# Scaling the attention probabilities inside their transposes: a diagonal right factor in place of row scalings

## The chip, the core and the metric

The kernel runs on one core of one Trainium2 chip. Its engines each work through a queue of their own in the order in which the program was built: TensorE (PE, with its weight loads shown apart as PEld), VectorE (DVE), ScalarE (ACT), GpSimd (POOL) and SyncE (SP), which issues most DMAs. An engine waits where an operand is not ready, and everything behind the waiting instruction waits with it. The metric is the device time of one execution in microseconds (us), median of three; lower is better.

## The reference

A sequence of 512 tokens of width 1024 goes through three layers in float32. The first has two kinds of attention (MLA with 8 heads, and SWA with 8 heads over a sliding window of 128), the second has 16 heads of attention with a forget bias (called "fox" below), and both are followed by a layer norm, an MLP, another layer norm and a gate. The third layer is gated linear attention and a gated MLP. What the change touches is the softmax of all 32 heads and the product with V:

```python
w = jax.nn.softmax(s, axis=-1).astype(v.dtype)
return jnp.einsum('bhqk,bkhd->bqhd', w, v)
```

## The kernel before

Tokens are cut into four blocks of 128 (`NB` = 4, `P` = 128). Large products run as three multiplies of split float32 (`mm3`: operands typed fp32r, held in the tiles `ar_t` and `ax_r`), while everything in plain float32 lies in `af_t` and `ax_f`. On PE, therefore, a row that names `ar_t` or `ax_r` is an fp32r multiply, a row that names only `af_t` and `ax_f` is a multiply of plain float32, and a row that names `ident` is a transpose (L255).

Each attention head is one generator, `head` (L758). For each block `i` of 128 queries it computes the scores (`smm`, in `layer1` or `layer2`), on DVE their row maximum (L808 or L812), on ACT the exponentials with their row sums `su` (`exps`, L794), and on DVE the reciprocal `rc` (L827). `preg(i)` is the region with the probabilities of query block `i`; it is 128 to 512 columns wide (128 or 256 in SWA). L828 and L829 scale each region by its row's reciprocal, four DVE instructions a head. Then PE transposes the 128x128 pieces of the regions, 7 a head in SWA and 10 a head in MLA and fox, so 8x7 + 8x10 + 16x10 = 296 in all, into two or three PSUM banks (`groups`); ACT alone, or ACT and DVE, copy the banks out (L840 to L846), and PE multiplies by V (L852 or L861). In SWA and MLA this last product is of plain float32, and so are MLA's scores; in fox both are fp32r.

The order on every engine is set when the program is built. `Core` keeps an estimated clock for each engine and estimated ready times for each stretch of memory; each operation is entered through a helper (`mm`, `tr`, `ts`, `tt`, ...) that adds its estimated cost to a clock, and `run` (L375) lets that generator go on whose next PE work is ready by these estimates, with a priority for older heads. A cost that is written differently thus moves instructions everywhere behind it. Buffers come from the arenas `R` (fp32r) and `F` (float32) through `alloc`, which makes a generator wait until there is room.

Of the kernel before, what the change touches and what calls it, by code (L numbers as in the profile page):

```python
# [9 lines left out]
F32 = mybir.dt.float32  # L10
F32R = mybir.dt.float32r
BF16 = mybir.dt.bfloat16
AF = mybir.ActivationFunctionType
ALU = mybir.AluOpType
# [4 lines left out]
NB = 4  # L19
P = 128  # L20
# [123 lines left out]
class Core:  # L144
# [91 lines left out]

    def mm(self, out, lhsT, rhs, start, stop, more=False):
        n = self.size(rhs)
        slow = 4 if rhs.dtype == F32 else 1
        m = self.size(lhsT)  # L240
        if rhs.dtype == F32R:
            cost = max((n + self.edge) / 2.4, 107 * m / 128)
        else:
            cost = slow * max(n / 2.39, 107 * m / (256 if rhs.dtype == BF16 else 128))
        self.op("pe", cost, [lhsT, rhs], [out])
        self.nc.tensor.matmul(out, lhsT, rhs, start=start, stop=stop, **(dict(skip_group_check=True) if more else {}))  # L246

# [307 lines left out]
def model_kernel(ctx: ExitStack, tc: tile.TileContext, a: dict, dbg=None):  # L555
# [13 lines left out]
    R, F = Arena(ar_t, NR), Arena(af_t, NF)  # L569
    c = Core(nc, R, F, Arena(sm_t, NS, 4), ps_t)  # L570
# [7 lines left out]
    def small(n):  # L578
        n4 = -(-n // 4) * 4
        if ring[0] + n4 > NS:  # L580
            ring[0] = 0
        o = ring[0]
        ring[0] += n4
        return sm_t[:, o : o + n]
# [4 lines left out]
    ident = cp.tile([P, P], F32, name="ident")  # L589
# [19 lines left out]
    def tb(t):  # L609
        return slice(t * P, t * P + P)  # L610
# [147 lines left out]
    def head(kind, qk, smm, scale, vst, of, orow, bias=None, init=None, sink=None, free=()):  # L758
# [19 lines left out]
        def preg(i):  # L778
            n, o = place[i]
            return pb[n].ap[:, o : o + width[i]]  # L780
# [5 lines left out]
        ng, su, rc = small(4), small(4), small(4)  # L786
# [16 lines left out]
        for n, bank in enumerate(banks):  # L803
            yield ("x", [c.pb(sb[n])])
            for i in bank:
                if bias is not None:
                    b = bias[:, 256 - width[i] : 256] if swa else bias[:, : width[i]]
# [17 lines left out]
        else:  # L825
            yield ("x", [su])
        c.vec(94, [su], [rc]).reciprocal(rc, su)  # L827
        for i in range(NB):  # L828
            c.ts(preg(i), preg(i), rc[:, i : i + 1])  # L829
        tset = yield from pl[1].get()  # L830
        tbk = []
        for grp in groups:
            yield ("pe", [preg(i) for _, i in grp], True)
            b = c.bank()
            for n, (j, i) in enumerate(grp):
                col = (0 if (j == i - 1 or i == 0) else 128) if swa else j * 128
                c.tr(c.pb(b)[:, n * 128 : n * 128 + 128], preg(i)[:, col : col + 128], ident)
            tbk.append((b, len(grp) * 128))
        pl[0].give(pset)
        for (b, w), tz in zip(tbk, tset):  # L840
            yield ("x", [c.pb(b)])
# [6 lines left out]
        if full:  # L848
            yield ("pe", [tz.ap for tz in tset] + [vst], True)
            b = c.bank()  # L850
# [5 lines left out]
        else:  # L856
            yield ("pe", [z.ap for tz in tset for z in tz[:2]] + [vst], True)
            b = c.bank()
# [121 lines left out]
    def layer1():  # L980
# [117 lines left out]
        def swa_pair(pr, b):  # L1098
            yield ("x", [c.pb(b)])
            of = yield from c.allocs(R, 512, 2)  # L1100
            po = PairOut(4 + pr, None, of)
            kv = pr // 2
            for hh in range(2):
                h = pr * 2 + hh
                qb = yield from c.alloc(R, 512)
                q = qb.ap
                own, oth = hh * 64, 64 - hh * 64
                src = c.pb(b)[own : own + 64]
                c.acopy(q[own : own + 64], src)
                c.tt(q[oth : oth + 64], src, f32(q[own : own + 64]), ALU.subtract)  # L1110

                def smm(out, i, q=q):
                    ks = slice(max(0, i - 1) * 128, i * 128 + 128)
                    c.mm(out, q[:, tb(i)], skh[kv][:, ks], True, False)
                    c.mm(out, q[:, tb(i)], skl[kv][:, ks], False, True)

                def fin(qb=qb, po=po):
                    qb.free()
                    po.one()
                    swa_done()  # L1120

                c.spawn(head("swa", [q, ske, bev], smm, 0.125, vsw[:, :, kv], of, own,
                             bias[:, h], nsink[:, h : h + 1], sink[:, h : h + 1], [fin]), prio())
            c.give(b)
# [72 lines left out]
        def mla_pair(pr, bq, bk):  # L1197
# [4 lines left out]
            for hh in range(2):  # L1202
                h = pr * 2 + hh
                yield ("x", [lambda: bool(kfree)])
                n = kfree.pop(0)
                k = kbb[n].ap
                qb = yield from c.alloc(F, 512)
                q = qb.ap
                rs = slice(hh * 64, hh * 64 + 64)
                rr = slice((h % 4) * 32, (h % 4) * 32 + 32)  # L1210
                c.acopy(k[0:64], c.pb(bk)[rs])
                c.act(q[0:64], c.pb(bq)[rs], AF.Copy, scale=96.0 ** -0.5)
                c.ts(q[64:96], rpb[h // 4].ap[rr], 96.0 ** -0.5)

                def smm(out, i, q=q, k=k):
                    c.mm(out, q[0:96, tb(i)], k[0:96, 0 : i * 128 + 128], True, False)
                    c.mm(out[:, i * 128 : i * 128 + 128], identb, maskb, False, True)

                def fin(qb=qb, n=n, po=po):
                    qb.free()  # L1220
                    kfree.append(n)
                    mla_done[0] += 1
                    po.one()

                c.spawn(head("mla", [q, k], smm, None, vm[:, :, h], of, hh * 64, free=[fin]), prio())
# [440 lines left out]
    def layer2():  # L1666
# [60 lines left out]
        def pair(pr, bq, bk):  # L1727
# [9 lines left out]
            for hh in range(2):  # L1737
# [22 lines left out]
                def fin(z=(qb, kb, lb, nb), po=po):  # L1760
# [3 lines left out]
                    if not vleft[g]:  # L1764
                        vb.free()
                    po.one()

                c.spawn(head("fox", [q, kh, kl], smm, 0.125, vst[:, :, (pr % 2) * 2 + hh], of, own, bias=nb.ap,
                             free=[fin]), prio())
            c.give(bq)  # L1770
# [715 lines left out]
```

## Time and profile before

| | before |
|---|---|
| median of 3 runs | 1842.64 us (1838.52 to 1843.07) |
| the profiled execution | 1841.28 us |
| its span from the first to the last instruction | 1839.6 us |
| PE busy | 1810.7 us (98%) |
| DVE busy | 1165.8 us (63%) |
| ACT busy | 901.0 us (49%) |

An engine's busy time is the union of its instructions' times. The mean time of one PE instruction is longer than its share of the engine, because multiplies overlap in the pipeline; what one costs is read from the distance between starts. In the timeline, instructions of one kind that follow each other are one row with their count, and the time of such a row reaches from the first start to the last end. "PEclk" is the clock granted to TensorE: 1.00 is 2.4 GHz, 0.50 is 1.2 GHz.

### The profile page before, as it was taken

How to read it: one execution, taken by the hardware profiler on the slowest of the kernel's cores; microseconds unless marked ns; L12 is line 12 of the kernel's file. 1: busy time of each engine (PE TensorE's matmuls, PEld its weight loads, DVE VectorE, ACT ScalarE, POOL GpSimd, SP SyncE). 2: the span in 40 equal slices, each digit the busy share in tenths (PEclk: the TensorE clock that was granted, in tenths of full speed). 3: DMA queues.
4: the chain of work that ended last, by engine and by line, in shares of the span. 5: the costliest groups of instructions: out<-in, count | busy, mean ns of one | idle time of the engine just before them, and what ended most of it. 6: DMA issues, size and time to landing. Idle time of an engine off the chain costs nothing. (4 is left out here: it accounts for less than half of the span.)

```text
span 1839.6 us, 23837 instructions
## 1 busy us (share of the span) xinstructions
PE 1810.7 (98%) x9096; PEld 1514.0 (82%) x9096; DVE 1165.8 (63%) x1939; ACT 901.0 (49%) x1594; POOL 141.3 (8%) x227
## 2 busy tenths in 40 slices
PE   9999999999999999999999999999999999999997
PEld 7776798888887888878888888878889898888886
DVE  4557667566568578778765656676675554634646
ACT  4567464545456365555655454563543243333434
POOL 1000011001011000000110100110010000100002
PEclk9999999999999999999999999999999999999999
DMA  5201256463663122323463646441222353633614
GB/s 174 76 32 55 95 183 162 104 193 77 186 137 99 53 93 70 115 69 115 164 168 104 182 93 195 97 142 64 81 92 81 126 189 98 150 125 81 172 24 98
DMA packets 63539, 212.01 MB, mean 115 GB/s; under 512 B 7544, under 2 KB 10160, under 8 KB 63424
## 3 DMA queue, kind: packets, MB, share of 16 engines
q1 hardware_dynamic: 50752, 165.39, 25.9%
q0 software_dynamic: 12672, 45.09, 14.1%
q8 instruction: 71, 1.16, 0.3%
q14 instruction: 44, 0.36, 0.1%
HBM read 208.32 MB, written 2.14 MB: 114 GB/s over the span
## 5 line engine op out<-in xcount | busy, mean ns | idle before, releaser
L246 PE MATMUL ps_t<-ar_t 128*128 128x512 f32 (+4 forms) x6537 | 1387.4, 367 | 9.7 <-DVE ar_t L294 3.3
L246 PEld LDWEIGHTS ps_t<-ar_t 128*128 128x128 f32 x6537 | 1127.5, 189 | 207.2 <-DVE ar_t L285 7.3
L285 DVE TENSOR_TENSOR ar_t<-af_t,ar_t 128x1024 fp32r<-128x1024 f32 (+4 forms) x450 | 457.6, 1034 | 356.1 <-ACT ar_t L274 353.4
L274 ACT CAST ar_t<-af_t 128x1024 fp32r<-128x1024 f32 (+4 forms) x477 | 412.1, 884 | 489.2 <-PE ps_t L246 329.1
L246 PE MATMUL ps_t<-ar_t,ax_r 128*128 128x512 f32 (+3 forms) x979 | 252.2, 387 | 0.4 <-ACT ax_r L274 0.2
L246 PEld LDWEIGHTS ps_t<-ar_t,ax_r 128*128 128x128 f32 (+1 forms) x979 | 180.4, 188 | 37.4 <-issue 1.0
L299 DVE SCALAR_TENSOR_TENSOR af_t<-af_t,ps_t 128x512 f32<-128x512 f32 (+2 forms) x218 | 138.1, 659 | 43.9 <-PE ps_t L246 37.8
L285 DVE TENSOR_TENSOR ar_t<-ps_t,ar_t 128x512 fp32r<-128x512 f32 (+4 forms) x181 | 104.3, 602 | 82.6 <-ACT ar_t L274 81.3
L274 ACT CAST ar_t<-ps_t 128x512 fp32r<-128x512 f32 (+4 forms) x181 | 88.4, 525 | 111.9 <-PE ps_t L246 48.7
L270 ACT ACTIVATE af_t<-af_t 128x512 f32<-128x512 f32 (+3 forms) x144 | 92.2, 643 | 103.5 <-DVE af_t L299 60.1
L285 DVE TENSOR_TENSOR ax_r<-af_t,ax_r 128x1024 fp32r<-128x1024 f32 (+4 forms) x109 | 90.9, 834 | 69.4 <-ACT ax_r L274 68.9
L274 ACT CAST ax_r<-af_t 128x1024 fp32r<-128x1024 f32 (+4 forms) x109 | 80.1, 738 | 86.4 <-PE ps_t L246 55.5
L285 DVE TENSOR_TENSOR af_t<-af_t 128x256 f32<-128x256 f32 (+2 forms) x228 | 99.3, 467 | 4.9 <-ACT af_t L270 2.1
L323 POOL DMA_DIRECT2D af_t<-in_w_down x64 | 55.4, 866 | 551.5 <-DVE ar_t L285 531.1
L246 PE MATMUL ps_t<-ax_r,ar_t 128*128 128x512 f32 (+5 forms) x451 | 97.0, 352 | 0.0
L246 PEld LDWEIGHTS ps_t<-ax_r,ar_t 128*128 128x128 f32 (+1 forms) x451 | 77.2, 187 | 12.2
L274 ACT COPY af_t<-ps_t 128x512 f32<-128x512 f32 (+3 forms) x108 | 58.7, 570 | 39.7 <-PE ps_t L246 25.6
L255 PE MATMUL ps_t<-ident,af_t 128*128 128x128 f32 (+1 forms) x499 | 69.2, 277 | 7.0 <-DVE af_t L299 6.9
L270 ACT ACTIVATE af_t<-af_t,sm_t 128x256 f32<-128x256 f32 (+4 forms) x92 | 60.6, 660 | 29.4 <-DVE sm_t L808 20.9
L255 PEld LDWEIGHTS ps_t<-ident,af_t 128*128 128x128 f32 (+1 forms) x499 | 58.7, 141 | 14.4 <-DVE af_t L299 8.1
L270 ACT ACTIVATE af_t<-ps_t 128x512 f32<-128x512 f32 (+3 forms) x111 | 58.7, 529 | 16.6 <-PE ps_t L246 16.4
L299 DVE SCALAR_TENSOR_TENSOR af_t<-af_t,sm_t 128x1024 f32<-128x1024 f32 x40 | 51.0, 1279 | 20.3 <-POOL sm_t L623 17.5
(99 smaller groups left out, 722.4 us busy)
## 6 DMA issues: line engine op xcount, KB each, us to landing
af_t<-in_w_up SPq DMA_DIRECT2D x64, 512.0 KB, 6.2
af_t<-in_w_down POOLq DMA_DIRECT2D x64, 512.0 KB, 5.5
af_t<-in_w_down SPq DMA_DIRECT2D x48, 512.0 KB, 5.4
af_t<-in_w_ffn_gate SPq DMA_DIRECT2D x22, 512.0 KB, 4.4
af_t<-in_w_ffn_up SPq DMA_DIRECT2D x22, 512.0 KB, 4.5
af_t<-in_w_ffn_down POOLq DMA_DIRECT2D x20, 512.0 KB, 5.5
af_t<-in_ple_w_gate SPq DMA_DIRECT2D x16, 512.0 KB, 3.8
af_t<-in_w_ffn_down SPq DMA_DIRECT2D x15, 512.0 KB, 3.4
```

The lines of the kernel that those rows point to most:

```text
L246: self.nc.tensor.matmul(out, lhsT, rhs, start=start, stop=stop, **(dict(skip_group_check=True) if more else {}))
L255: self.nc.tensor.transpose(out, src, ident)
L270: self.nc.scalar.activation(out, src, func, **kw)
L274: self.nc.scalar.copy(out, src)
L285: self.nc.vector.tensor_tensor(out, a, b, op=op)
L299: self.nc.vector.scalar_tensor_tensor(out, a, s, b, op0=op0, op1=op1)
L323: self.nc.gpsimd.dma_start(out, src, accum_op=ALU.add)
```

## The change

The four row scalings of a head go. In their place a DVE instruction multiplies the 128x128 identity, repeated four times, by the four columns of `rc`, which gives four diagonal matrices in a new buffer `dg` of 512 columns. Each transpose becomes a plain multiply with the same stationary operand (the piece of the probabilities, not scaled) and the diagonal of its query block as the moving operand, so that transposing and scaling are one product. The buffer is freed after the last of them. Besides, the planner's price of a plain float32 multiply in `mm` is written anew: n x 0.84 + 4 ns for n columns, where it was four times the larger of n / 2.39 and 107 m / 128 ns (m is the number of stationary columns).

```diff
     def mm(self, out, lhsT, rhs, start, stop, more=False):
         n = self.size(rhs)
-        slow = 4 if rhs.dtype == F32 else 1
...
-            cost = slow * max(n / 2.39, 107 * m / (256 if rhs.dtype == BF16 else 128))
+            cost = n * 0.84 + 4 if rhs.dtype == F32 else max(n / 2.39, 107 * m / 256)
...
         c.vec(94, [su], [rc]).reciprocal(rc, su)
-        for i in range(NB):
-            c.ts(preg(i), preg(i), rc[:, i : i + 1])
+        dgb = yield from c.alloc(F, 512)
+        dg = dgb.ap
+        c.tt(dgb.v(4), ident.unsqueeze(1).to_broadcast([P, NB, P]), rc.unsqueeze(2).to_broadcast([P, NB, P]), ALU.mult)
         tset = yield from pl[1].get()
         tbk = []
         for grp in groups:
-            yield ("pe", [preg(i) for _, i in grp], True)
+            yield ("pe", [preg(i) for _, i in grp] + [dg[:, tb(i)] for _, i in grp], True)
             b = c.bank()
             for n, (j, i) in enumerate(grp):
                 col = (0 if (j == i - 1 or i == 0) else 128) if swa else j * 128
-                c.tr(c.pb(b)[:, n * 128 : n * 128 + 128], preg(i)[:, col : col + 128], ident)
+                c.mm(c.pb(b)[:, n * 128 : n * 128 + 128], preg(i)[:, col : col + 128], dg[:, tb(i)], True, True)
             tbk.append((b, len(grp) * 128))
+        dgb.free()
         pl[0].give(pset)
```

On DVE, the end of one of the last fox heads' softmax stands like this before (the first two rows are a weight's low part and the sum of a residual):

```order
L285 TENSOR_TENSOR ar_t<-af_t,ar_t 128x1024
L299 SCALAR_TENSOR_TENSOR af_t<-af_t,ps_t 128x512
L827 RECIPROCAL sm_t<-sm_t 128x4
L290 TENSOR_SCALAR af_t<-af_t,sm_t 128x128
L290 TENSOR_SCALAR af_t<-af_t,sm_t 128x256
L290 TENSOR_SCALAR af_t<-af_t,sm_t 128x384
L290 TENSOR_SCALAR af_t<-af_t,sm_t 128x512
```

And now, at the same place:

```order
L284 TENSOR_TENSOR ar_t<-af_t,ar_t 128x1024
L284 TENSOR_TENSOR af_t<-ps_t,af_t 64x512
L298 SCALAR_TENSOR_TENSOR af_t<-af_t,ps_t 128x512
L826 RECIPROCAL sm_t<-sm_t 128x4
L284 TENSOR_TENSOR af_t<-ident,sm_t 128x512
```

One instruction of 512 columns stands where there were four of 128 to 512. (Line numbers shift by one.)

On PE, in layer 1, where the first two SWA heads (and three pieces of a latent vector) are transposed between fp32r multiplies of 384 columns, the order before is:

```order
L246 MATMUL ps_t<-ar_t 128x384 x12
L255 MATMUL ps_t<-ident,ax_f 128x128 x12
L255 MATMUL ps_t<-ident,af_t 128x128 x2
L255 MATMUL ps_t<-ident,ax_f 128x128
L255 MATMUL ps_t<-ident,af_t 128x128 x2
L246 MATMUL ps_t<-ar_t 128x384 x6
L246 MATMUL ps_t<-af_t,ax_f 64x256 x3
L246 MATMUL ps_t<-af_t,ax_f 64x128
```

And now (the rows of 128x128 that name only `ax_f` and `af_t` are the new products with the diagonal; the one with `ident` is a transpose that stays):

```order
L245 MATMUL ps_t<-ar_t 128x384 x6
L245 MATMUL ps_t<-ax_f 128x128 x4
L254 MATMUL ps_t<-ident,ax_f 128x128 x3
L245 MATMUL ps_t<-ax_f 128x128 x3
L245 MATMUL ps_t<-ar_t 128x384 x6
L245 MATMUL ps_t<-ax_f 128x128 x2
L245 MATMUL ps_t<-ax_f,af_t 128x128 x2
L245 MATMUL ps_t<-af_t,ax_f 64x256 x3
L245 MATMUL ps_t<-af_t,ax_f 64x128
```

One stretch of 17 transposes has become several stretches of plain float32 multiplies, with fp32r multiplies between them.

On PE, near the end of layer 2: the rows of 512 columns (`x36` and `x12` before) are the 48 multiplies that project q and k of the last pair of heads but one, the rows of 512, 384, 128 and 256 columns in twos are products with V, and the first row of 128 columns in twos begins this pair's scores. Before:

```order
L246 MATMUL ps_t<-ar_t 128x512 x36
L255 MATMUL ps_t<-ident,af_t 128x128 x20
L246 MATMUL ps_t<-ar_t 128x512 x12
L246 MATMUL ps_t<-ax_r,ar_t 128x512 x2
L246 MATMUL ps_t<-ax_r,ar_t 128x384 x2
L246 MATMUL ps_t<-ax_r,ar_t 128x128 x2
L246 MATMUL ps_t<-ar_t 128x256 x2
L246 MATMUL ps_t<-ar_t 128x512 x2
L246 MATMUL ps_t<-ar_t 128x384 x2
L246 MATMUL ps_t<-ar_t 128x128 x2
L246 MATMUL ps_t<-ar_t 128x256 x2
L246 MATMUL ps_t<-ar_t 128x128 x2
```

And now:

```order
L245 MATMUL ps_t<-af_t 128x128 x20
L245 MATMUL ps_t<-ar_t 128x512 x18
L245 MATMUL ps_t<-ax_r,ar_t 128x512 x2
L245 MATMUL ps_t<-ax_r,ar_t 128x384 x2
L245 MATMUL ps_t<-ax_r,ar_t 128x128 x2
L245 MATMUL ps_t<-ar_t 128x256 x2
L245 MATMUL ps_t<-ar_t 128x512 x2
L245 MATMUL ps_t<-ar_t 128x384 x2
L245 MATMUL ps_t<-ar_t 128x128 x2
L245 MATMUL ps_t<-ar_t 128x256 x2
L245 MATMUL ps_t<-ar_t 128x512 x24
L245 MATMUL ps_t<-ar_t 128x128 x2
```

Here 24 multiplies precede the 20 products with the diagonal, so that 24 + 18 + 6 of the last-but-one row make this pair's projection, and the other 18 of that row are the next pair's; they now stand between the projection and the scores that need it.

## Rows read from the trace of the kernel before

**Rows 1.** The page: span, and busy time by engine.
```profile
span 1839.6 us, 23837 instructions
PE 1810.7 (98%) x9096; PEld 1514.0 (82%) x9096; DVE 1165.8 (63%) x1939; ACT 901.0 (49%) x1594; POOL 141.3 (8%) x227
```

**Rows 2.** Busy us and instructions by stretch: attention of layers 1, 2; an MLP.
```profile
core 0: us, PE busy (x) PEld busy (x) DVE busy (x) ACT busy (x) POOL busy (x), PEclk, DMA share, GB/s
57.00:216.00 159.00, 154.97 (x766) 113.14 (x765) 98.94 (x243) 93.87 (x232) 2.41 (x6) 0.99 0.23 72
596.00:890.00 294.00, 289.26 (x1673) 248.94 (x1672) 216.93 (x462) 157.75 (x337) 7.67 (x12) 0.99 0.28 90
...
300.00:360.00 60.00, 60.00 (x266) 49.66 (x266) 36.30 (x50) 30.35 (x43) 1.93 (x3) 1.00 0.55 163
```

**Rows 3.** Transposes, by shape: count, busy us, mean ns; and 20 in the timeline.
```profile
L255 PE MATMUL ps_t<-ident,af_t 128*128 128x128 f32 x491 | 68.0, 277 | 7.0 <-DVE af_t L299 6.9
L255 PE MATMUL ps_t<-ident,ax_f 128*128 128x128 f32 x121 | 19.0, 277 | 0.0
...
798.45 2.35 PE L255 MATMUL ps_t<-ident,af_t 128*128 128x128 f32 x20
```

**Rows 4.** Plain float32 multiplies, MLA scores: start us, us, instruction; then by shape.
```profile
92.28 0.45 PE L246 MATMUL ps_t<-ax_f 96*128 96x128 f32 x2
92.57 0.22 PE L246 MATMUL ps_t<-maskb,identb 128*128 128x128 bf16 x1
...
93.94 1.07 PE L246 MATMUL ps_t<-ax_f 96*128 96x512 f32 x2
94.85 0.22 PE L246 MATMUL ps_t<-maskb,identb 128*128 128x128 bf16 x1
...
121.96 0.39 PE L246 MATMUL ps_t<-ax_f 96*128 96x128 f32 x2
122.18 0.22 PE L246 MATMUL ps_t<-maskb,identb 128*128 128x128 bf16 x1
...
L246 PE MATMUL ps_t<-ax_f 96*128 96x512 f32 x8 | 4.3, 619 | 0.0
L246 PE MATMUL ps_t<-af_t,ax_f 96*128 96x512 f32 x8 | 4.2, 612 | 0.0
```

**Rows 5.** Weight loads (PEld), by shape: transposes, then plain float32 of MLA scores.
```profile
L255 PEld LDWEIGHTS ps_t<-ident,af_t 128*128 128x128 f32 x491 | 58.0, 142 | 13.9 <-DVE af_t L299 8.1 <-DVE af_t L285 0.5 <-issue 0.4
L246 PEld LDWEIGHTS ps_t<-ax_f 96*128 96x128 f32 x32 | 4.9, 191 | 1.5 <-issue 0.7 <-ACT ax_f L270 0.2 <-ACT af_t L274 0.2
```

**Rows 6.** Timeline of PE: two stretches of plain float32 with what follows.
```profile
63.34 3.24 PE L246 MATMUL ps_t<-af_t,ax_f 128*64 128x256 f32 x16
66.52 0.55 PE L255 MATMUL ps_t<-ident,ax_f 128*128 128x128 f32 x3
...
111.93 2.37 PE L246 MATMUL ps_t<-af_t 128*64 128x512 f32 x8
114.23 7.12 PE L246 MATMUL ps_t<-ar_t 128*128 128x512 f32 x30
```

**Rows 7.** DVE by shape: a row scaling, and a product of two SBUF operands.
```profile
L285 DVE TENSOR_TENSOR af_t<-af_t 128x512 f32<-128x512 f32 x42 | 28.8, 689 | 3.0 <-ACT af_t L270 2.1
...
L290 DVE TENSOR_SCALAR af_t<-af_t,sm_t 128x512 f32<-128x512 f32 x24 | 11.6, 482 | 4.6 <-POOL sm_t L728 4.6
...
L290 DVE TENSOR_SCALAR af_t<-af_t,sm_t 128x128 f32<-128x128 f32 x16 | 4.6, 287 | 0.6
```

**Rows 8.** Timeline near the end of layer 2, then one stretch as in Rows 2.
```profile
803.38 1.13 PE L246 MATMUL ps_t<-ax_r,ar_t 128*128 128x512 f32 x6
...
806.77 1.06 ACT L274 CAST ar_t<-ps_t 64x512 fp32r<-64x512 f32 x2
...
809.38 0.57 PE L246 MATMUL ps_t<-ar_t 128*128 128x128 f32 x2 [3.31 <-DVE ar_t L294]
...
811.00:814.60 3.60, 3.60 (x11) 2.68 (x10) 3.51 (x11) 1.10 (x5) 0.00 (x0) 0.53 0.00 0
```

## The prediction

> **What bounds the kernel now.** I read the page first. PE is busy 1810.7 of 1839.6 us, DVE 63% of it [rows 1]. A busy PE could still be one that waits inside its pipeline, so the next view is the busy time by stretch, for the two stretches in which the changed code runs. In the attention of layer 1 PE is idle 159.0 - 155.0 = 4.0 us, in that of layer 2 294.0 - 289.3 = 4.7 us, while DVE has 60 and 77 us to spare [rows 2]. So time that is taken off DVE can give back 8.7 us at the very most, and only where DVE is what PE waits for; time that is put on PE is paid in full. The question is what the change puts on PE.
>
> **Part 1: DVE.** Four scalings a head go, of 0.29 us (128 columns) to 0.48 us (512) [rows 7]; with the other widths in proportion a head of MLA or fox spends 1.54 us on them and one of SWA (128 columns and three times 256) 1.34, so 24 x 1.54 + 8 x 1.34 = 48 us in all. One product of 512 columns comes, 0.69 us by the row of the same size [rows 7], so 32 x 0.69 = 22 us. DVE is relieved of some 26 us, and the way from the reciprocal to PE gets some 0.7 us shorter. Since PE doesn't wait there before, I cost both at nothing; what hides them is the fp32r work that the planner puts between a head's scores and its transposes. ACT's copies out of the banks stay what they are.
>
> **Part 2: PE, 296 transposes become multiplies.** A transpose: 20 of them in a row take 2.35 us, of which the last one's own length is 0.27, so (2.35 - 0.27) / 19 = 0.109 us from start to start [rows 3]. The trace has one record for each: 491 + 121 [rows 3], as many as the program has.
>
> The trace of before has no plain float32 multiply of this very shape (128 x 128 stationary, 128 moving columns), but it has near ones, in MLA's scores (96 rows, 128 stationary columns). There the thing to see is the count: a single multiply of the program shows as "x2", and the eight multiplies of 512 columns (one a head) have 8 + 8 = 16 records [rows 4]. So a plain float32 multiply goes through the array twice, and its weights are loaded twice. Its price is the distance from its first start to the start of what follows: 92.57 - 92.28 = 0.29 us for 128 columns behind fp32r work, 122.18 - 121.96 = 0.22 us for 128 columns behind transposes, 94.85 - 93.94 = 0.91 us for 512 [rows 4]. The slope is (0.91 - 0.29) / 384 = 1.61 ns a column, so 0.21 us for 128. A long run of products with V, 14 times 128 columns from 63.34 to 66.52, gives 3.18 / 14 = 0.227 [rows 6]. I take 0.22, from the row of the same width with weights as wide. The bounds are 0.207 and 0.29 us.
>
> The double price of the load must be looked at too: a plain float32 load of 128 columns takes 191 ns against a transpose's 142 [rows 5]. In the row that I use (0.22 us for two passes) both loads are in, so they overlap with the passes; with 128 rows instead of 96 nothing in the trace says otherwise.
>
> The sum: 296 x (0.22 - 0.109) = **+32.9 us** (29 to 35 by 0.207 and 0.227; the 0.29 belongs to single multiplies with a changeover on either side, which is part 3). All of it lies on the engine that sets the end.
>
> A rule of the skill goes further. The Trainium skill, "TensorE: Matmul & The Clock Gate", section "Terms", says that the transpose mode is four times faster for FP32. That speaks against the change, as the rows do, but harder: 4 x 0.109 = 0.436 us for a multiply would make the sum 296 x 0.327 = 97 us. The rows above show a factor of two, and the measurement decides; what is left of the rule is in the third rival.
>
> **Part 3: changeovers.** A run of plain float32 costs more than its columns. From 111.93 to 114.23 there are 1280 columns, 2.30 us where 1.61 ns a column give 2.06: 0.24 more. The 30 fp32r multiplies behind it take 7.12 us; without the last one's tail of about 0.39 that is 6.73 for 29 distances, where an MLP has 60 / 266 = 0.2256 us each, so 6.54: another 0.19 [rows 2, 6]. A run between fp32r work thus costs 0.2 to 0.43 us extra. In the order of the program I count 17 stretches off fp32r work with plain float32 in them before, and 33 now (fox has eight of 20 products in one, and four of 10, where there was none). 16 x 0.2 to 16 x 0.43 is 3.2 to 6.9; I take **+4 us**, nearer the lower end, since part 2's 0.22 already holds a share of it.
>
> **Part 4: what moves.** Both the new products and the new price shift the plan. The new price, 0.84 ns a column, is half of the slope above, so in the plan PE runs faster than it does on the chip. That costs nothing by itself: the other engines' results, due by a fast PE, are early for a slow one, and a wait of ACT or DVE for PE does not delay PE. It rather makes PE's waits shorter.
>
> The one long wait of PE in attention stands at 809.38: 3.31 us for the last copies of q and k (DVE L294) [rows 8]. PE had only 2.7 us of products with V behind the projection (from 803.38 on), and ACT began with q and k at 806.77 only, after copying those products' results. Behind the wait, the stretch from 811.0 to 814.6 has a granted clock of 0.53, so mostly 1.2 GHz in place of 2.4, while PE is busy without a break [rows 8]: about 3.6 x 0.47 = 1.7 us more. Now the products with V stand ahead of the projection's end, and 18 multiplies of the next pair, 18 x 0.2256 = 4.1 us, stand between it and the scores. From 806.77 to 809.38 the preparation took 2.6 us; that is covered. If it took all of the 6.0 us from 803.38, a wait of 1.9 us would be left. I take the wait and the slow clock as gone, **-5.0 us** (0 to -5). New waits may come from the reordering; I have no row for one and keep them for the range.
>
> **The sum.** From the profiled execution, 1841.28 us, 32.9 + 4 - 5 gives 1873.2. That execution lies 1.4 us below the median of the runs, so the median after should be near **1874 us**, 1.7% slower.
>
> **The rivals.** (a) *Not slower: the diagonal product costs what the new price says.* 128 x 0.84 + 4 = 111.5 ns, as much as a transpose. It would be so if the two records of a plain float32 multiply were one multiply seen twice. Then parts 2 and 3 vanish, only -5 us is left, and the time is about 1838 us; it decides from a price below about 0.127 us a product (296 x 0.018 = 5.3 us). Against it: the distances to the next instruction, not the records alone, hold both passes [rows 4]. If DVE's relief took PE's other waits in attention as well (8.7 us in all, with 1.7 of slow clock), it would be 1832.
> (b) *The reordering opens waits.* A wait like that at 809.38, with the slow clock behind it, costs 5 us [rows 8]. That one staying and one or two more coming makes 1879 to 1889 us. For it: every order on every engine changed. Against it: part 4's reason.
> (c) *The products cost more than twice a transpose*, because 128 rows and new weights for every 128 columns leave the loads bare: two of 191 ns [rows 5] are 0.38 us, 296 x 0.273 = 81 us, and the time about 1920 us. The factor of four that the Trainium skill names would give 1841 + 97 = 1938, in the same direction; the rows speak against both.
>
> **How the numbers follow.** The forecast with its own small variations gets 0.68, (b) 0.18, (a) 0.09 (0.06 near 1838, 0.03 near 1832), (c) 0.05. The low end is 0.207 us a product, 3 us of changeovers, the wait gone and 3 us of the other waits too: 1842.6 + 29 + 3 - 5 - 3 = 1867, and some more for what I have not seen, 1862. The high end is 1842.6 + 35 + 7, the wait as it is, and one new one of 5 us: 1890. These hold (b) for the most part, and leave out (a) and (c), 0.14. Slower by over 0.3% (5.5 us, about what a measurement of this kernel can tell from no change): 0.88; within 0.3%: 0.08; faster: 0.04.
>
> **What the profile after would show.** If part 2 is right, the transposes' group shrinks by 296 records, a group of plain float32 multiplies of 128*128 by 128x128 has 592, and 20 products in a row take about 4.4 us where the transposes took 2.35. PE's idle time stays at or below 29 us, so that the added time is added busy time. If part 1 is right, DVE's busy time falls by about 26 us and nothing answers to that. If part 4 is right, no wait of PE for DVE L293 of over 2 us stands before the last pairs' scores, and no stretch of low clock follows there. A product with the diagonal at 0.11 us, or 20 in a row at 7 us or more, would make the prediction wrong from its main term.

## The result, and the profile after

The changed kernel takes 1875.12 us (median; 1874.52 to 1878.82), the kernel before 1842.12: a ratio of 1.0178, with a 95% interval of 1.0166 to 1.019. It is 33.0 us slower; 31.4 were forecast from the median that was known then. The page of the changed kernel (span, and busy time by engine):

```profile
span 1872.9 us, 24345 instructions
PE 1844.9 (99%) x9392; PEld 1549.7 (83%) x9392; DVE 1152.4 (62%) x1843; ACT 904.8 (48%) x1594; POOL 140.5 (8%) x227
```

Against [rows 1] the span is 33.3 us longer, PE's busy time 34.2 us longer, and PE's idle time (span less busy) goes from 28.9 to 28.0. By this view all of the loss is busy time of PE and none is waiting; busy time also holds what work takes longer at the low clock (below). PE has 296 instructions more, 9392 against 9096. The groups of 128x128 by line and shape say what they are (count, busy us and mean ns of one):

```profile
L245 PE MATMUL ps_t<-af_t 128*128 128x128 f32 x360 | 43.6, 275 | 0.0
L254 PE MATMUL ps_t<-ident,af_t 128*128 128x128 f32 x299 | 41.7, 278 | 6.2 <-DVE af_t L298 6.2
L245 PE MATMUL ps_t<-af_t,ax_f 128*128 128x128 f32 x144 | 19.9, 281 | 0.5 <-DVE af_t L284 0.5
L245 PE MATMUL ps_t<-ax_f 128*128 128x128 f32 x64 | 9.0, 278 | 0.0
L245 PE MATMUL ps_t<-ax_f,af_t 128*128 128x128 f32 x24 | 4.0, 275 | 0.0
L254 PE MATMUL ps_t<-ident,ax_f 128*128 128x128 f32 x17 | 3.0, 271 | 0.0
```

The transposes went from 612 [rows 3] to 316, and 296 products have 360 + 144 + 64 + 24 = 592 records: two each, called passes below. What a run of 20 costs is read from its start to the start of what follows. After, in layer 2 (start us, us, instruction):

```profile
711.54 4.62 PE L245 MATMUL ps_t<-af_t 128*128 128x128 f32 x40
...
715.93 2.98 PE L245 MATMUL ps_t<-ar_t 128*128 128x512 f32 x12
```

And what follows the 20 transposes of [rows 3] in the kernel before:

```profile
800.55 2.99 PE L246 MATMUL ps_t<-ar_t 128*128 128x512 f32 x12
```

20 products take 715.93 - 711.54 = 4.39 us, 0.220 each; 20 transposes took 800.55 - 798.45 = 2.10, 0.105 each. The 12 fp32r multiplies behind either run are alike (2.98 and 2.99 us), so the changeover is no dearer behind products than behind transposes. Layer 1 agrees: its first 10 products of an MLA head (first two lines, after) take 105.56 - 103.41 = 2.15 us, and 10 transposes of such a head (last two lines, before) take 101.36 - 100.35 = 1.01.

```profile
103.41 2.39 PE L245 MATMUL ps_t<-af_t,ax_f 128*128 128x128 f32 x20
105.56 1.87 PE L245 MATMUL ps_t<-ar_t 128*128 128x128 f32 x11
...
100.35 1.25 PE L255 MATMUL ps_t<-ident,ax_f 128*128 128x128 f32 x10
101.36 5.03 PE L246 MATMUL ps_t<-ar_t 128*128 128x512 f32 x21
```

By the two runs of 20 the change adds 296 x (4.39 - 2.10) / 20 = 33.9 us to PE; the busy time grew by 34.2.

Two smaller things came out otherwise than forecast. The wait at 809.38 us [rows 8], which stood before the seventh of the eight pairs of fox heads, is gone; before that pair's scores PE now goes on without a break:

```profile
834.49 7.38 PE L245 MATMUL ps_t<-ar_t 128*128 128x256 f32 x36
841.71 0.23 PE L245 MATMUL ps_t<-maskb,identb 128*128 128x128 bf16 x1
```

But the third pair now waits in the same way. In the timeline of the changed kernel:

```profile
719.71 3.10 PE L245 MATMUL ps_t<-ar_t 128*128 128x256 f32 x16
...
721.36 1.05 ACT L273 CAST ar_t<-af_t 128x1024 fp32r<-128x1024 f32 x1 [0.52 <-PE ps_t L245]
722.44 1.06 ACT L273 CAST ax_r<-ps_t 64x512 fp32r<-64x512 f32 x2
...
725.71 0.72 PE L245 MATMUL ps_t<-ax_r 128*128 128x128 f32 x2 [2.89 <-DVE ax_r L293]
...
728.95 2.91 PE L245 MATMUL ps_t<-ar_t 128*128 128x512 f32 x6
731.66 0.52 PE L245 MATMUL ps_t<-ar_t,ax_r 128*128 128x128 f32 x2
```

And the stretch behind the wait (columns as in [rows 2], PEclk third from the end):

```profile
725.40:732.20 6.80, 6.50 (x22) 5.02 (x22) 5.75 (x16) 3.00 (x9) 0.00 (x0) 0.50 0.37 137
```

PE has only the products with V behind the projection, and ACT begins with q and k only at 722.44, behind a weight's cast; PE waits 2.89 us for DVE's copies. Behind the wait the granted clock is 0.50 (1.2 GHz) for 6.8 us. Six multiplies of 512 columns take 731.66 - 728.95 = 2.71 us there, 0.45 each, twice the 0.2256 of an MLP [rows 2]; so the low clock costs, by estimate, half of the 6.8 us, another 3.4 us. And DVE's busy time fell by 13.4 us, not by 26.

### The profile page after: what moved, and what is told of

Same layout as the page of the kernel before. It is cut to its first block, busy times and chain, and to the rows that moved or that the text cites. A ratio compares the mean times of both kernels' runs of the same rounds, so it can differ in the third digit from the quotient of the medians.

```text
span 1872.9 us, 24345 instructions
## 1 busy us (share of the span) xinstructions
PE 1844.9 (99%) x9392; PEld 1549.7 (83%) x9392; DVE 1152.4 (62%) x1843; ACT 904.8 (48%) x1594; POOL 140.5 (8%) x227
## 5 line engine op out<-in xcount | busy, mean ns | idle before, releaser
L245 PE MATMUL ps_t<-ar_t,ax_r 128*128 128x512 f32 (+3 forms) x1003 | 259.4, 387 | 0.5 <-ACT ax_r L273 0.2
L245 PEld LDWEIGHTS ps_t<-ar_t,ax_r 128*128 128x128 f32 (+1 forms) x1003 | 185.7, 189 | 39.2 <-issue 0.8
L298 DVE SCALAR_TENSOR_TENSOR af_t<-af_t,ps_t 128x512 f32<-128x512 f32 (+2 forms) x218 | 138.1, 659 | 43.1 <-PE ps_t L245 36.7
L298 DVE SCALAR_TENSOR_TENSOR af_t<-af_t,sm_t 128x1024 f32<-128x1024 f32 x40 | 50.9, 1279 | 20.8 <-POOL sm_t L622 15.3
L245 PE MATMUL ps_t<-af_t 128*128 128x128 f32 (+4 forms) x420 | 62.7, 301 | 0.0
L284 DVE TENSOR_TENSOR af_t<-ps_t,af_t 128x512 f32<-128x512 f32 (+1 forms) x66 | 45.2, 685 | 25.2 <-PE ps_t L245 14.1
```

The lines of the kernel that those rows point to most:

```text
L284: self.nc.vector.tensor_tensor(out, a, b, op=op)
L298: self.nc.vector.scalar_tensor_tensor(out, a, s, b, op0=op0, op1=op1)
```

## Experiments

Every ratio below is to the kernel before, which ran beside it on the same chip, with its 95% interval.

**Is it the products' own time?** The changed kernel's plan is kept, on every engine, and only what PE does at the 296 places is altered.

```diff
-                c.mm(c.pb(b)[:, n * 128 : n * 128 + 128], preg(i)[:, col : col + 128], dg[:, tb(i)], True, True)
+                c.op("pe", 128 * 0.84 + 4, [preg(i)[:, col : col + 128], dg[:, tb(i)]], [c.pb(b)[:, n * 128 : n * 128 + 128]])
+                nc.tensor.transpose(c.pb(b)[:, n * 128 : n * 128 + 128], preg(i)[:, col : col + 128], ident)
```

> The changed kernel with its 296 products by the diagonal put back to transposes by the identity, entered in the plan at the product's price, so that every engine's order stays that of the changed kernel; the diagonals are still made on DVE and nothing reads them (the probabilities are not scaled). Theory (the product's own time on PE is the whole loss): 296 x (0.222 - 0.1095) = 33 us come back, 1875 - 33 = 1842 us, 1837 to 1847. Rival (the new order, with its waits, is the loss): stays within 6 us of 1875.

1842.73 us, ratio 0.9999 (0.9989 to 1.001). Its page:

```profile
span 1844.6 us, 23742 instructions
PE 1814.7 (98%) x9096; PEld 1518.3 (82%) x9096; DVE 1150.5 (62%) x1843; ACT 901.0 (49%) x1594; POOL 140.5 (8%) x227
```

PE is busy 30.2 us less than in the changed kernel (in the profiled execution, which at 1846.33 us was the longest of ten), and DVE, which still makes the diagonals, does the same. In the new order, with the transposes back, the kernel is as fast as before: by the medians 32.4 us return, 0.109 us a product. The rival that the new order is the loss falls.

The opposite: each product twice.

```diff
+                nc.tensor.matmul(c.pb(b)[:, n * 128 : n * 128 + 128], preg(i)[:, col : col + 128], dg[:, tb(i)], start=True, stop=True)
                 c.mm(c.pb(b)[:, n * 128 : n * 128 + 128], preg(i)[:, col : col + 128], dg[:, tb(i)], True, True)
```

> The changed kernel with each of the 296 products issued twice into the same place, the second not entered in the plan, so that the order is otherwise the same. Theory (a product is two passes, 0.222 us): 1875 + 296 x 0.222 = 1941 us, less the few us of PE's waits that this covers, 1932 to 1942. Rival (a product costs what its price in the planner says, 0.1115 us): 1875 + 33 = 1908 us.

1939.55 us, ratio 1.0522 (1.0503 to 1.0542). 64.4 us for 296 more products is 0.218 us each, twice the planner's 0.1115. The new price counts one pass of two. The Trainium skill ("TensorE: Matmul & The Clock Gate", section "Terms") calls the transpose mode four times faster for FP32, and does not say than what. Against a plain float32 multiply of the same size a transpose is two times faster here, 0.105 to 0.109 us against 0.218.

**Is it one kind of head?** One half of the heads keeps the products, the other gets its row scalings and transposes back. The condition `full` is true for MLA and SWA, so in the kernel that ran it is the 160 products of fox that stay:

```diff
-        dgb = yield from c.alloc(F, 512)
...
+        if full:
+            for i in range(NB):
+                c.ts(preg(i), preg(i), rc[:, i : i + 1])
+        else:
+            dgb = yield from c.alloc(F, 512)
...
-                c.mm(c.pb(b)[:, n * 128 : n * 128 + 128], preg(i)[:, col : col + 128], dg[:, tb(i)], True, True)
+                if full:
+                    c.tr(c.pb(b)[:, n * 128 : n * 128 + 128], preg(i)[:, col : col + 128], ident)
+                else:
+                    c.mm(c.pb(b)[:, n * 128 : n * 128 + 128], preg(i)[:, col : col + 128], dg[:, tb(i)], True, True)
```

> The changed kernel with the products in the 16 fox heads (layer 2) taken back and their row scalings and transposes put in again; the 136 products of layer 1 (MLA and SWA) stay. Theory (a product costs 0.11 us more than a transpose wherever it stands): 1843 + 136 x 0.112 = 1858 us, 1853 to 1863 with what the order does. Rival (the loss is where DVE and PE wait for each other in layer 2): near 1843; or, were it in layer 1 alone, near 1875.

I had the two halves the wrong way round in that text: it describes the mirror of this kernel. By the same theory, 160 products make 1843.8 + 160 x 0.112 = 1862 us, and the rivals change places (near 1843 if layer 1 were all of the loss, near 1875 if layer 2 were). Measured: 1859.36 us, ratio 1.0083 (1.0068 to 1.0098). The page shows the 160 added passes (9256 against 9096) and 18.5 us more of busy time than [rows 1]:

```profile
span 1857.5 us, 24122 instructions
PE 1829.2 (98%) x9256; PEld 1533.3 (83%) x9256; DVE 1160.6 (62%) x1891; ACT 903.2 (49%) x1594; POOL 140.0 (8%) x227
```

By the medians the 160 products of fox cost 15.5 us over the kernel before, 0.097 each, and the 136 of layer 1 the remaining 15.8, 0.116 each. By PE's busy time they cost 18.5 us, 0.116 each, and 1844.9 - 1829.2 = 15.7 us, 0.115 each. Both halves pay, by number and not by place; that the medians give fox 2 us less is within what orders were seen to differ by (below).

**Is DVE's relief worth anything?** The kernel before without its row scalings, in the same order.

```diff
         for i in range(NB):
-            c.ts(preg(i), preg(i), rc[:, i : i + 1])
+            c.op("dve", c.vcost(width[i], True) + 62, [preg(i), rc[:, i : i + 1]], [preg(i)])
```

> The kernel before with its 128 row scalings left out (the probabilities stay unscaled); the plan still counts them, so that every engine's order is the same without them. DVE has 48 us less to do. Theory (PE waits for DVE almost nowhere): 1842 us, at most 5 us less if the wait at 809 us and its low clock go, 1836 to 1844. Rival (DVE's relief is worth something where PE waits for it): the whole 8.7 us of idle time in the two attentions and 1.7 us of low clock come back, 1832 us.

1841.41 us, ratio 0.9991 (0.9982 to 1.0001): no difference that the interval tells from none, and PE's wait of 3.3 us for q and k stays. Its page:

```profile
span 1838.4 us, 23705 instructions
PE 1810.7 (98%) x9096; PEld 1515.2 (82%) x9096; DVE 1128.7 (61%) x1811; ACT 900.8 (49%) x1594; POOL 141.4 (8%) x227
```

DVE has 1165.8 - 1128.7 = 37.1 us less to do than in [rows 1], and PE is as busy as before, to the tenth. Also, the scalings were worth 37 us and not the 48 that I had added up from mean times: in a row they overlap, as a line of the kernel before shows (four scalings of 128 to 512 columns, whose mean times add up to 1.54):

```profile
845.84 1.27 DVE L290 TENSOR_SCALAR af_t<-af_t,sm_t 128x128 f32<-128x128 f32 x4
```

**What is the planner's price worth?** First on the kernel before, the new price alone:

```diff
-        slow = 4 if rhs.dtype == F32 else 1
...
-            cost = slow * max(n / 2.39, 107 * m / (256 if rhs.dtype == BF16 else 128))
+            cost = n * 0.84 + 4 if rhs.dtype == F32 else max(n / 2.39, 107 * m / 256)
```

> The kernel before (row scalings, transposes) with the planner's new price of plain float32 alone, 0.84 ns a column; only the order differs. Theory (the products are the loss, the price is not): within 5 us of 1843. Rival (half the true price spoils the plan and is a part of the loss): 1848 us or more.

1842.8 us, ratio 0.9995 (0.9985 to 1.0004): nothing, in a program with 103 plain float32 multiplies (206 records). For 128 by 128 by 128 the old formula gives 428 ns and the new one 111.5, about twice and half of the measured 0.218 to 0.220 us. Then in the changed kernel, where 296 more hang on the price:

```diff
-            cost = n * 0.84 + 4 if rhs.dtype == F32 else max(n / 2.39, 107 * m / 256)
+            cost = n * 1.68 + 4 if rhs.dtype == F32 else max(n / 2.39, 107 * m / 256)
```

> The changed kernel with the planner's price of plain float32 at 1.68 ns a column in place of 0.84; only the order differs. Theory (the order is worth little, the products are the loss): 1868 to 1880 us. Rival (the half price misleads the plan and opened the wait of 2.9 us and the 6.8 us at the low clock near 725 us): these go, 1875 - 6 = 1869 us or less, and PE has no wait of over 2 us in the attention of layer 2.

1865.36 us, ratio 1.0125 (1.0109 to 1.0141): 9.8 us less than the changed kernel, the same instructions in another order. The page:

```profile
span 1863.9 us, 24350 instructions
PE 1841.8 (99%) x9392; PEld 1550.7 (83%) x9392; DVE 1152.1 (62%) x1843; ACT 903.9 (48%) x1594; POOL 139.8 (8%) x227
```

And PE's waits (us in total, times, longest):

```profile
PE ps_t L254 <- DVE af_t L298: 3.6, 2, 1.8
PE ps_t L245 <- ACT ar_t L273: 3.4, 3, 1.7
...
PE ps_t L245 <- DVE ar_t L293: 1.5, 1, 1.5
```

PE's idle time is 22.1 us in place of 28.0, and it is busy 3.1 us less. In the changed kernel the first and the last of these waits were:

```profile
PE ps_t L254 <- DVE af_t L298: 6.2, 3, 2.3
...
PE ps_t L245 <- DVE ax_r L293: 2.9, 1, 2.9
```

So the waits for q and k (L293) and those for a norm's result (L298) are 4.0 us less together, most of the 5.9 us of idle time; the rest of the gain is busy time. My theory that the order is worth little was wrong by these 10 us, and the rival's forecast held (1869 us or less, no wait of over 2 us in the attention of layer 2). Is it the true price that does it, or the luck of one order? The same line with 1.26, 1.47 and 2.10:

> The changed kernel with the planner's price of plain float32 at 1.26 ns a column (0.84 in the changed kernel, 1.68 in the run that took 1865 us). If a price nearer the truth makes a better plan step by step: between 1865 and 1875 us, about 1870. If the 10 us are the luck of one order: anywhere within 6 us of 1870, with no line through the prices.

> As before, at 1.47 ns a column. Step by step: about 1867 us, and below the run with 1.26. Luck of one order: anywhere from 1864 to 1876 us, and the runs with 1.26, 1.47, 1.68 and 2.10 don't lie in a row.

> As before, at 2.10 ns a column, above the truth. If the true price is what makes the plan good: above 1865 us, about 1870. If a plan that takes PE for slower than it is leaves no waits: 1865 us or less. Luck of one order: anywhere from 1864 to 1876 us.

| price, ns a column | 0.84 (the change) | 1.26 | 1.47 | 1.68 | 2.10 |
|---|---|---|---|---|---|
| median, us | 1875.12 | 1865.9 | 1859.79 | 1865.36 | 1868.78 |
| ratio to before | 1.0178 | 1.0119 | 1.0085 | 1.0125 | 1.0136 |
| 95% interval | 1.0166 to 1.019 | 1.0104 to 1.0134 | 1.0068 to 1.0102 | 1.0109 to 1.0141 | 1.0120 to 1.0151 |

All four prices about the measured one (0.218 to 0.220 us for 128 columns, 1.70 to 1.72 ns a column) beat the half price, by 6 to 15 us. Among them there is no line: 1.47 lies 5.6 us under 1.68, though 1.68 is nearer the truth. It also lies below both of its forecasts, though one of its four executions took 1864.0 us; 1.26 and 2.10 fit either of theirs. That the order of the half price is worse than these four orders is shown; that half the price is the reason is not, since it is one order too, and the four differ among themselves by 9 us. The wait at 725.71 is not the whole of it: in the order of 2.10 the same wait stands, before another pair, and that kernel is still 6.3 us faster than the change.

```profile
PE ps_t L245 <- DVE ax_r L293: 2.9, 1, 2.9
```

Why 1.47 is best stays open. None of these orders pays for the products: the best is still 0.85% slower than the kernel before.

**Do the better orders help without the products?** In the order of 1.68, the products become transposes, as in the first experiment:

> The changed kernel planned with 1.68 ns a column for plain float32, and its 296 products put back to transposes, entered at the product's price, so that the order is that of the run with 1.68; the diagonals are made and not read (the probabilities are not scaled). If the 10 us that the better price gave belong to the order alone: 1865 - 33 = 1832 us. If they need PE to be as slow as that plan takes it to be: 1840 us or more, as PE then runs ahead of the plan and waits.

1835.14 us, ratio 0.9952 (0.9937 to 0.9967), between the two forecasts and nearer the first. 30.2 us return, and the order keeps most of its worth with PE quicker than its plan takes it to be. With the scalings in it, it is a kernel that computes what the reference asks:

```diff
-        c.tt(dgb.v(4), ident.unsqueeze(1).to_broadcast([P, NB, P]), rc.unsqueeze(2).to_broadcast([P, NB, P]), ALU.mult)
+        c.op("dve", c.vcost(512, False), [rc] + [preg(i) for i in range(NB)], [dg])
+        for i in range(NB):
+            nc.vector.tensor_scalar_mul(preg(i), preg(i), rc[:, i : i + 1])
```

> As the run before it, and the four row scalings stand in DVE's queue where the product of the identity and the reciprocals was (entered at that product's price), so that it computes what the kernel before does, in the other order. If DVE has the 26 us to spare there: as the run before it, 1832 us, faster than the kernel before. If not: 1840 us or more, with waits of PE for the transposed regions.

1838.29 us, ratio 0.997 (0.9958 to 0.9981), again between the forecasts: 3.2 us more than the run before it. Among PE's waits is one that the run before it does not have, of the transposes (L840 in this kernel) for DVE, whose four scalings take longer than the one product that they stand for:

```profile
PE ps_t L840 <- DVE ar_t L284: 2.1, 2, 1.8
```

And the same in the order of 1.47:

> The four row scalings and the transposes put into the order of the run with 1.47 ns a column, as was done for 1.68 in e10_scalings_in_order; it computes what the kernel before does. If the order keeps its worth with quicker PE work in it: 1859.8 - (1865.4 - 1838.3) = 1833 us, a ratio of 0.994 to the kernel before. If the order of 1.47 was good only with the products' slow PE: 1838 us or more.

1836.27 us, ratio 0.996 (0.9947 to 0.9974): 0.4% faster than the kernel before, and by its median the fastest that computes the whole (its interval overlaps that of the order of 1.68). It is 3 us above the first forecast and 2 below the second. Its page:

```profile
span 1833.1 us, 23848 instructions
PE 1808.7 (99%) x9096; PEld 1513.1 (83%) x9096; DVE 1165.7 (64%) x1939; ACT 902.1 (49%) x1594; POOL 139.6 (8%) x227
```

Every engine has as many instructions as in [rows 1]; PE's idle time is 24.4 us in place of 28.9, and its busy time 2.0 less. With the products, the orders of 1.68 and 1.47 were worth 9.8 and 15.3 us against the order of the change, which with transposes is as fast as the kernel before. Without the products, and computing the whole, they are worth 5.6 and 7.6 us against the kernel before: over half of it, and half.

## Why the prediction was right, and where it was not

**The main term was right, in mechanism and size.** Part 2 gave +32.9 us: 296 products of 0.22 us for transposes of 0.109. Measured were 0.220 us in a run of 20, 0.218 in the run with each product twice, and 32.4 us between products and transposes in one and the same order. The step that carried it was the count of records: "x2" in the timeline for one multiply of the program [rows 4]. The rival that a product costs what its price says (0.1115 us) took that record for the whole multiply; the rival with bare weight loads (0.38 us) is excluded by the same runs.

**Part 3 was mis-sized: +4 us were forecast, and next to nothing came.** Its 0.2 to 0.43 us a run were read at products with V, which have 64 stationary columns [rows 6], and were taken to belong to plain float32. Runs of 20 products with 128 stationary columns show 4.39 us for 40 passes, 0.110 us each, and in layer 1 10 products cost 2.15 - 1.01 = 1.14 us more than 10 transposes, 0.114 each: no extra beside the products' own time. The fp32r multiplies behind them go on as behind transposes (2.98 and 2.99 us for 12), so what they lose at a changeover they lost before the change too. What the extra time behind the products with V hangs on, the width or something else, was not tried.

**Part 4 was right on the one wait and wrong on the total: -5 us were forecast, and none of it is left.** The wait at 809.38 us did go, for the reason given. But rival (b) took place beside it: a wait of the same kind and nearly the same size opened four pairs of heads earlier, with a longer stretch at the low clock. (By its own price of 5 us a wait, (b) should have reached from 1884 to 1889 us with one or two new waits beside the old one, not from 1879; here one wait took the other's place.) PE's idle time was 28.9 and is 28.0 us, and the low clock behind the new wait costs, by estimate, 3.4 us where that behind the old one cost 1.7. The errors of parts 3 and 4 have opposite signs and cancel, so the nearness of the total (1874 forecast, 1875 measured) is partly luck.

**Part 4's costing of the half price at nothing did not hold.** Its reason, that the other engines' results "are early for a slow one", says that PE's waits get shorter; PE's idle time was 28.0 us in this order and 22.1 in that of 1.68, with the same products. The order that came with the half price is 6 to 15 us worse than four others. Against the kernel before it lost nothing by itself, as the first experiment shows (0.9999 with transposes); what it missed is what better orders gain. Whether a price nearer the truth makes the better order by rule is not shown.

**Part 1 was right where it mattered and mis-sized where it did not.** DVE's relief was costed at nothing, and taking the scalings away whole is worth nothing that can be measured (0.9991, 0.9982 to 1.0001). Its size was 13.4 us, not 26: the scalings were 37 us and not 48, because mean times of instructions that overlap were added up, and the products come to 37.1 - 13.4 = 23.7 us, near the 22 forecast.

## What to carry to other kernels

Where PE is busy 98% of the span, as here, work that moves from an engine with time to spare onto PE is paid in full, however short it makes the other engine's queue; look first for the engine that sets the end. Before a price is read from a trace, count its records against the program's instructions: a plain float32 multiply shows as two, each with half the time, and a planner that is given one of them is wrong by a factor of two. And where a planner sets the order, try a few values of a price about the measured one: here the order alone moved the same work by up to 15 us.

## What the runs showed that was not expected

A transpose of 128x128 float32 costs 0.105 us in a run and a plain float32 multiply of the same size 0.220, although its two weight loads, new for every product, take 192 ns each by their own records. These are the loads of the largest group of products (count, busy us, mean ns), and the run of 20 from 711.54 us on (columns as in [rows 2]):

```profile
L245 PEld LDWEIGHTS ps_t<-af_t 128*128 128x128 f32 x360 | 42.3, 192 | 0.4
...
711.54:715.93 4.39, 4.39 (x42) 4.38 (x40) 2.16 (x4) 2.15 (x5) 0.00 (x0) 1.00 0.59 208
```

The loads overlap with the passes, and with each other: 40 of 192 ns would be 7.7 us one after the other, and the run took 4.39. By the slope of 1.61 ns a column from the prediction the passes alone would take 0.207 us, an estimate, so by it the loads add some 0.01 us. But PEld is busy for 4.38 of the 4.39 us, as PE is; which of the two sets the pace is not shown. A wait of 2.89 us was followed by 6.8 us at the low clock, so that the wait cost more behind it (3.4 us, by estimate) than by itself. And four orders of the same instructions, from prices between 1.26 and 2.10, differ by 9 us, over a quarter of what the change itself costs.
